# Casts held for a VectorE instruction, and a new work order, in a batched attention kernel

## The chip, the cores and the metric

The kernel runs on one core of a Trainium2 chip. The metric is the device time of one launch in microseconds (us), as the median of several runs; lower is better. The core has five engines with a queue of instructions each, which run beside one another and meet only at semaphores: TensorE (PE; its weight loads are listed as PEld), VectorE (DVE), ScalarE (ACT), GpSimd (POOL) and SyncE (SP), which here only issues transfers.

## The reference

Softmax attention for 8 batches of 8 heads, with 512 queries and keys of 64 elements, in float32:

```python
scale = 1.0 / np.sqrt(q.shape[-1])
scores = np.einsum('bhqd,bhkd->bhqk', q, k) * scale
scores = scores - scores.max(axis=-1, keepdims=True)
attn = np.exp(scores)
attn = attn / attn.sum(axis=-1, keepdims=True)
return np.einsum('bhqk,bhkd->bhqd', attn, v).astype(np.float32)
```

The 64 heads are independent. The kernel does not subtract the maximum; the division by the sum comes at the end.

## The kernel before

**Tiling.** Two heads form a pair, 32 pairs g in all; of each pair q, k and v are loaded as float32 tiles of 128 partitions by 512 elements. Scores are computed transposed: a unit (g, c, h) is a block of 128 keys (chunk c of four) by the 512 queries of head h, so a head has four units and the kernel 256. Of these, 14 (chunk 0 of the first head of the pairs listed in ASIDE) are not given to ScalarE. The other 242 are packed into 83 tiles: the first ones of 1, 1 and 2 units, the last of 1, and 79 of three. A tile is three banks of PSUM, and two such tiles exist (tag `ps_st`).

**The steps.** Each of them is a letter in a string ORDER, which `work` (L333) walks from left to right; each letter issues its instructions to the engines' queues in that order.
- `s`, a tile (L281): three score matmuls on TensorE (L180), one exponential over the tile on ScalarE (L227, `pt<-st`), and, when a pair's first tile is two back, the loads of q and k eight pairs on and of v six pairs on, from SyncE's queue (L97).
- `c`, a cast (L305): on GpSimd, q, then k of a pair to float16 (L115), or v of the pair two before into the value tile `vp` (L121), in a fixed sequence.
- `t`, a turn (L297): eight transposes on TensorE of a pair's cast q and k into one bank of PSUM (L138), and VectorE's copy out of it (L139, `tqk<-tps`).
- `h`, a head (L292): sixteen matmuls on TensorE of the exponentials with the values and a column of ones (L239), then on VectorE the reciprocal of the sums (L252) and the product (L253, `osb<-o,rcp`); after a pair's second head SyncE stores the pair (L261).
- `a`, an aside (L316): one score matmul (L197), and on VectorE the start of an exponential made of arithmetic: an integer part n (L199) and a fraction f (L203, reading PSUM and n). `e` (L323) is its power of two on GpSimd (L207), and `p` (L326) one of three passes on VectorE (L203): `a<-f`, `f<-f,e` and `pa<-a,f`. Each of these passes reads two tensors from SBUF (the first reads f twice). The passes give the unit's weights, which the head of that unit uses last.

**What orders the work.** An engine executes its queue strictly in the order in which ORDER issued it, with no planner at run time. Between engines only data and buffers bind: a turn needs its casts, scores need their turn's copy and a free one of the two score tiles, so the exponential two tiles back; a head needs its exponentials and values. Turns, heads and asides share two banks of PSUM (tag `ps_x`), taken in order, so TensorE can start the next of these only when VectorE has emptied the one two before it. Six value tiles exist, so v of pair g is cast after the heads of pair g - 6. Before ORDER stands a hand-written opening (L340 to L396) for pairs 0 and 1; after it `close` (L275) computes the last head. GpSimd's queue holds only casts and powers, and runs as far ahead as loads and buffers let it.

Of the kernel before, what the change touches and what calls it, by code (L numbers as in the profile page):

```python
# [25 lines left out]

ASIDE = (2, 4, 8, 9, 12, 13, 16, 17, 20, 21, 25, 26, 28, 30)
ORDER = (  # L30
    "csctsccchcacstpshecshpsctchcscccastcepcsctshpcchcstsphcsctpcschccasetshsccpcchhcpshctstacc"
    "shpshstpshhccccstaschesccpaschcepcsctcshscphhpccststesphaschcpsccthsptshscepchaschcsphsttc"
    "cescphpcschapcscchshpccstshpscehashcpshtstcscpthpecshcshtsccphcapccsshhpsctshcccsphceashsp"
    "ccchsttpshaeccshpstcshpshhpscchpsehtsptasshpshhpshcsephhpshshshh"
)


# [1 line left out]
def kernel(  # L39
# [11 lines left out]
    nc = tc.nc  # L51
# [12 lines left out]
    for g in range(n_pairs):  # L64
# [3 lines left out]
        else:  # L68
            units += [(g, c, h) for c in range(NI) for h in range(2)]
    aside = [(g, 0, 0) for g in ASIDE]  # L70
    units = [u for u in units if u not in aside]
# [37 lines left out]
    vps = [cpool.tile([P, 2, NI, W], FP16, name=f"vp{n}") for n in range(NV)]  # L109
    halves, tqk, turned = {}, {}, {}  # L110

    def cast_half(g, n, eng=nc.gpsimd.tensor_copy):
        if g not in halves:
            halves[g] = xpool.tile([P, 2, NI, P], FP16, tag="qk", name=f"qk_{g}", bufs=6)
        eng(  # L115
            out=halves[g][:, n].rearrange("p i (h d) -> p i h d", d=D),
            in_=raw[g, "qk"[n]].rearrange("p h (i d) -> p i h d", d=D),
        )

    def cast_v(g):  # L120
        nc.gpsimd.tensor_copy(  # L121
            out=vps[g % NV][:, :, :, 0:D],
            in_=raw[g, "v"].rearrange("p h (i d) -> p h i d", d=D),
        )

    def aux(shape, dt, name):
        return pspool.tile(shape, dt, tag="ps_x", bufs=2, name=name)

    def transpose(g, parts=(0, 1)):
        if g not in turned:  # L130
            turned[g] = xpool.tile([P, 2, S], FP16, tag="tqk", name=f"tqk_{g}")
            for h in range(2):
                tqk[g, h] = [turned[g][D * h : D * (h + 1), n] for n in range(2)]
        lo, hi = parts[0], parts[-1] + 1
        ps = aux([P, hi - lo, NI, P], FP16, f"tps_{g}_{lo}")
        for n in parts:
            for i in range(NI):
                nc.tensor.transpose(ps[:, n - lo, i, :], halves[g][:, n, i, :], ident16)  # L138
        nc.vector.tensor_copy(out=turned[g][:, lo:hi], in_=ps)  # L139

    N = 2 * NI
    FIRST = NI - 1
# [41 lines left out]
    class Aside:  # L184
# [5 lines left out]
        def __init__(self, unit):  # L190
            self.unit, self.g = unit, unit[0]
            g, c, h = unit
            tq, tk = tqk[g, h]
            n, e, f, a = self.tmp("n", I8), self.tmp("e", I32), self.tmp("f"), self.tmp("a")
            res = self.tmp("pa", FP16)
            s = aux([P, S], FP32, f"sa_{g}")
            nc.tensor.matmul(s, tk[:, c * P : (c + 1) * P], tq, start=True, stop=True)  # L197
            rate = 2.0 * scale * LOG2E
            nc.vector.tensor_scalar(  # L199
                out=n, in0=s, scalar1=rate, scalar2=SHIFT, op0=AluOp.mult, op1=AluOp.add  # L200
            )
            def step(o, x, k, y, op0=AluOp.add, op1=AluOp.mult):
                nc.vector.scalar_tensor_tensor(out=o, in0=x, scalar=k, in1=y, op0=op0, op1=op1)  # L203

            step(f, s, rate, n, AluOp.mult, AluOp.subtract)
            def power():
                nc.gpsimd.tensor_scalar(  # L207
                    out=e,
                    in0=n,
                    scalar1=float(1 << 22),  # L210
                    scalar2=float(LEAD_BITS),
                    op0=AluOp.mult,
                    op1=AluOp.add,
                )

            self.power = power
            self.passes = deque([
                lambda: step(a, f, EXP_P, f),
                lambda: step(f, f, EXP_R, e.bitcast(FP32)),
                lambda: step(res, a, EXP_Q, f),  # L220
            ])
            self.res = res
# [25 lines left out]
    def normalise(g, h, o, lo=0, hi=NI):  # L248
        if g not in o_sb:
            o_sb[g] = opool.tile([P, 2, NI, D], FP32, tag="o_sb", name=f"osb_{g}")  # L250
        rcp = opool.tile([P, NI], FP32, tag="rcp", name=f"rcp_{g}_{h}_{lo}")
        nc.vector.reciprocal(out=rcp[:, lo:hi], in_=o[:, lo:hi, D:W])  # L252
        nc.vector.tensor_tensor(  # L253
            out=o_sb[g][:, h, lo:hi],
            in0=o[:, lo:hi, 0:D],
            in1=rcp[:, lo:hi].broadcast_to([P, hi - lo, D]),
            op=AluOp.mult,
        )

    def save(g, h, n):  # L260
        nc.sync.dma_start(  # L261
# [4 lines left out]
    def attend(g, h):  # L266
        o = aux([P, NI, W], FP32, f"o_{g}_{h}")
        weigh(g, h, o)
        normalise(g, h, o)
        if g == last:  # L270
            save(g, h, 1)
        elif h == 1:
            save(g, 0, 2)

    def close():  # L275
        o = pspool.tile([P, NI, W], FP32, tag="ps_st", bufs=2, name="o_last")
        weigh(last, 1, o)
        normalise(last, 1, o)
        save(last, 1, 1)
# [17 lines left out]
    def turns():  # L297
        for n in range(2):
            transpose(1, (n,))
            yield  # L300
        for g in range(2, n_pairs):
            transpose(g)
            yield

    def casts():  # L305
        for g in range(2, n_pairs + LAG):
            for n in range(2 if g < n_pairs else 0):
                cast_half(g, n)
                yield
            if g >= LAG:  # L310
                cast_v(g - LAG)
                yield
# [19 lines left out]

    def work(order):  # L333
        steps = {k: f().__next__ for k, f in zip("shtca", (tiles, heads, turns, casts, asides))}
        steps |= {"e": next_power, "p": next_pass}
        for k in order:
            steps[k]()

    with tc.manual_schedule():
# [53 lines left out]
        softmax(0)  # L393
        softmax(1)
        cast_half(1, 0, Y)
        cast_half(1, 1, V)  # L396
        work("stst" + ORDER)
        close()

# [28 lines left out]
```

## Time and profile before

| quantity | value |
|---|---|
| median of 5 runs | 121.27 us (120.92 to 121.63) |
| the profiled execution's own time | 121.57 us |
| its span, first to last instruction | 119.8 us |
| ScalarE busy | 111.4 us (93%) |
| TensorE busy, matmuls | 108.1 us (90%) |
| VectorE busy | 102.6 us (86%) |
| GpSimd busy | 71.0 us (59%) |
| read from HBM, written | 25.17 MB, 8.39 MB |
| granted TensorE clock | 1.00 |

How to read the lines. A line of the groups names the source line, the engine, the operation, then out<-in by the program's names, shapes and the number of instructions; behind it stand busy time in us and the mean of one in ns, and behind the last bar the idle time of the engine just before them with what ended it. A line of the waits says which engine at which line waited for what: us in total, times, longest. A line of a timeline has the start and the length in us of one instruction or of a merged run of equal ones, and in brackets idle time before it. The chain of waits is followed back from the last instruction: start, us, what; "issue" is time in which the engine waited for nothing that the profile shows.

### The profile page before, as it was taken

The numbers are of one execution on the slowest core, as the hardware profiler recorded it, in microseconds if no ns is written. First come the engines' busy times: TensorE is split into PE (matmuls) and PEld (weight loads), VectorE is DVE, ScalarE is ACT, GpSimd is POOL, SyncE is SP. The second block draws the span as 40 slices with busy tenths as digits, with TensorE's granted clock in tenths as the row PEclk, the third lists the DMA queues.
The fourth block names the chain that finished last, engine by engine and source line by source line (L and its number), as shares of the span: only waits on it lengthen the run. The fifth ranks groups of instructions, "written<-read, shape, count | busy, mean of one in ns | idle before, by whom it ended". The sixth has DMA issues, their size and how long they took to land.

```text
span 119.8 us, 4065 instructions
## 1 busy us (share of the span) xinstructions
PE 108.1 (90%) x1585; PEld 65.1 (54%) x1585; DVE 102.6 (86%) x246; ACT 111.4 (93%) x88; POOL 71.0 (59%) x114
## 2 busy tenths in 40 slices
PE   6979897989999998999989999999899899979970
PEld 6734554555654645546645565566555566536560
DVE  1354999799999899989999999998999899999870
ACT  4569999999999999999999999999999999999950
POOL 2148899997867869874785577916678424220000
PEclk9999999999999999999999999999999999999999
DMA  3999999999999999999988999899999812404334
GB/s 101 314 345 353 351 346 348 354 376 373 355 356 292 352 360 339 353 376 372 310 262 269 361 345 332 245 358 323 317 333 323 270 47 78 165 5 143 123 109 157
DMA packets 34882, 33.81 MB, mean 282 GB/s; under 512 B 2096, under 2 KB 34864, under 8 KB 34864
## 3 DMA queue, kind: packets, MB, share of 16 engines
q1 hardware_dynamic: 34576, 33.30, 84.8%
q8 instruction: 12, 0.20, 0.7%
q10 hardware_dynamic: 288, 0.26, 0.6%
q14 instruction: 6, 0.05, 0.1%
HBM read 25.17 MB, written 8.39 MB: 280 GB/s over the span
## 4 chain that ended last, share of the span: by engine, by line
ACT 65%; issue 16%; PE 9%; DMA 4%; DVE 1%; SPq 1%; POOL 1%
ACT pt L227 65%; PE o L239 4%; DMA q<-in_q_dram 4%; PE st L180 4%; DVE osb L253 1%; SPq L104 1%; POOL qk L115 1%; DVE rcp L252 0%; PE tps L138 0%
## 5 line engine op out<-in xcount | busy, mean ns | idle before, releaser
L227 ACT ACTIVATE pt<-st 128x1536 f16<-128x1536 f32 (+2 forms) x83 | 109.0, 1496 | 1.5 <-PE st L180 1.2
L180 PE MATMUL st<-tqk 64*128 64x512 f16 x234 | 47.6, 381 | 3.6 <-ACT pt L227 2.5
L239 PEld LDWEIGHTS <-pt 128*128 128x128 f16 x968 | 33.4, 97 | 23.4 <-issue 13.1
L239 PE MATMUL o<-vp,pt 128*128 128x65 f16 x952 | 38.8, 194 | 1.7 <-DVE osb L253 0.6
L121 POOL CAST vp<-v 128x512 f16<-128x512 f32 x32 | 20.9, 655 | 18.3 <-PE o L239 8.5
L253 DVE TENSOR_TENSOR osb<-o,rcp 128x256 f32<-128x256 f32 x63 | 26.8, 425 | 2.2
L115 POOL CAST qk<-q 128x512 f16<-128x512 f32 x31 | 20.6, 663 | 8.3 <-DMA q<-in_q_dram 7.7
L139 DVE COPY tqk<-tps 128x1024 f16<-128x1024 f16 (+1 forms) x32 | 21.3, 669 | 3.2 <-PE tps L138 3.0
L115 POOL CAST qk<-k 128x512 f16<-128x512 f32 x30 | 22.3, 745 | 0.9 <-DMA k<-in_k_dram 0.4
L138 PEld LDWEIGHTS <-qk 128*128 128x128 f16 x248 | 14.4, 97 | 12.9 <-issue 5.4
L138 PE MATMUL tps<-ident,qk 128*128 128x128 f16 x248 | 19.1, 219 | 1.5 <-POOL qk L115 0.7
L180 PEld LDWEIGHTS <-tqk 64*128 64x128 f16 x234 | 11.1, 93 | 11.0 <-issue 3.7
L252 DVE RECIPROCAL rcp<-o 128x4 f32<-128x4 f32 x63 | 11.1, 176 | 3.2 <-PE o L239 2.5
L207 POOL TENSOR_SCALAR e<-n 128x512 int32<-128x512 int8 x14 | 8.7, 620 | 4.8 <-DVE n L199 3.8
L203 DVE SCALAR_TENSOR_TENSOR f<-f,e 128x512 f32<-128x512 f32 x14 | 10.8, 771 | 0.0
L203 DVE SCALAR_TENSOR_TENSOR pa<-a,f 128x512 f16<-128x512 f32 x14 | 10.4, 740 | 0.0
L203 DVE SCALAR_TENSOR_TENSOR f<-sa,n 128x512 f32<-128x512 f32 x14 | 9.7, 691 | 0.5
L203 DVE SCALAR_TENSOR_TENSOR a<-f 128x512 f32<-128x512 f32 x14 | 9.9, 708 | 0.0
L199 DVE TENSOR_SCALAR n<-sa 128x512 int8<-128x512 f32 x14 | 9.5, 681 | 0.0
L197 PE MATMUL sa<-tqk 64*128 64x512 f16 x14 | 5.4, 385 | 0.1
L239 PE MATMUL o<-vp,pa 128*128 128x65 f16 x56 | 4.0, 193 | 0.0
L366 PE MATMUL warm<-blank 128*128 128x128 f16 x25 | 2.8, 313 | 1.0 <-DVE small L348 1.0
(36 smaller groups left out, 23.8 us busy)
## 6 DMA issues: line engine op xcount, KB each, us to landing
v<-in_v_dram SPq DMA_DIRECT2D x32, 256.0 KB, 5.8
q<-in_q_dram SPq DMA_DIRECT2D x31, 256.0 KB, 5.9
k<-in_k_dram SPq DMA_DIRECT2D x31, 256.0 KB, 5.9
out_dram<-osb SPq DMA_DIRECT2D x31, 256.0 KB, 5.3
raw<-in_k_dram ACTq DMA_DIRECT2D x2, 128.0 KB, 3.0
raw<-in_q_dram SPq DMA_DIRECT2D x2, 128.0 KB, 2.8
out_dram<-osb SPq DMA_DIRECT2D x2, 128.0 KB, 1.9
```

The lines of the kernel that those rows point to most:

```text
L115: eng(out=halves[g][:, n].rearrange("p i (h d) -> p i h d", d=D), in_=raw[g, "qk"[n]].rearrange("p h (i d) -> p i h d", d=D),)
L121: nc.gpsimd.tensor_copy(out=vps[g % NV][:, :, :, 0:D], in_=raw[g, "v"].rearrange("p h (i d) -> p h i d", d=D),)
L138: nc.tensor.transpose(ps[:, n - lo, i, :], halves[g][:, n, i, :], ident16)
L139: nc.vector.tensor_copy(out=turned[g][:, lo:hi], in_=ps)
L180: nc.tensor.matmul(st[j][:, x, :], key, tq, start=True, stop=True)
L199: nc.vector.tensor_scalar(out=n, in0=s, scalar1=rate, scalar2=SHIFT, op0=AluOp.mult, op1=AluOp.add)
L203: nc.vector.scalar_tensor_tensor(out=o, in0=x, scalar=k, in1=y, op0=op0, op1=op1)
L207: nc.gpsimd.tensor_scalar(out=e, in0=n, scalar1=float(1 << 22), scalar2=float(LEAD_BITS), op0=AluOp.mult, op1=AluOp.add,)
L227: nc.scalar.activation(out=pt[j][:, 0:n], in_=st[j][:, 0:n], func=EXP, scale=scale)
L239: nc.tensor.matmul(o[:, i, :], p[:, i * P : (i + 1) * P], vps[g % NV][:, h, c, :], start=(c == chunks[0] and i == 0), stop=(c == chunks[-1 ...
L252: nc.vector.reciprocal(out=rcp[:, lo:hi], in_=o[:, lo:hi, D:W])
L253: nc.vector.tensor_tensor(out=o_sb[g][:, h, lo:hi], in0=o[:, lo:hi, 0:D], in1=rcp[:, lo:hi].broadcast_to([P, hi - lo, D]), op=AluOp.mult,)
```

## The change

ASIDE and ORDER are replaced: the 14 units computed aside now belong to other pairs, and the 388 letters stand in another order, with 54 of a new letter `w` among them. All other letters occur as often as before (92 c, 79 s, 63 h, 42 p, 30 t, 14 a, 14 e). A `w` notes the VectorE instruction that was last issued by a turn (its copy), an aside or a pass (its last scalar_tensor_tensor) or a head (its product); the next cast that is issued is made to wait until that instruction is done. A second `w` before that cast replaces the note. Nothing else of the kernel is touched.

```diff
-ASIDE = (2, 4, 8, 9, 12, 13, 16, 17, 20, 21, 25, 26, 28, 30)
+ASIDE = (2, 5, 7, 11, 12, 13, 17, 18, 20, 22, 23, 26, 28, 30)
 ORDER = (
-    "csctsccchcacstpshecshpsctchcscccastcepcsctshpcchcstsphcsctpcschccasetshsccpcchhcpshctstacc"
-    "shpshstpshhccccstaschesccpaschcepcsctcshscphhpccststesphaschcpsccthsptshscepchaschcsphsttc"
-    "cescphpcschapcscchshpccstshpscehashcpshtstcscpthpecshcshtsccphcapccsshhpsctshcccsphceashsp"
-    "ccchsttpshaeccshpstcshpshhpscchpsehtsptasshpshhpshcsephhpshshshh"
+    "cccscscthscasctewcpwschhswccphstwcscpccwtchshashpshcsecctwpwwstcchpshcwstccacscehstwspthcc"
+    "wcpshwcspchtccschaswtccpshcewsacwshwspchwheswptspchwspcchtcsacschpwceshtcpcshshwscpttcwwps"
+    "cwchccshwacecshstchwspchccastwwpsetswwpchshwscphhwpcshcacswscphtespwtcsctswcphchwccspchwaw"
+    "schspehccasscwhwsptcwhwcpstsctwwtcwwcspcheapwcschpshesctschwashcpwststsphhsphewcpwshaeshps"
+    "tshpshphschwcpshphshwcswhhsh"
 )
...
+    latest, held = [], []
+    behind = mybir.DependencyInfo(mybir.DependencyClass.Sync, mybir.DependencyReason.DATA)
+
+    def hold(ins):
+        if held:
+            tc.add_manual_dep(ins.ins, held.pop().ins.name, behind, reason="shared SBUF port")
...
-        eng(
+        ins = eng(
             out=halves[g][:, n].rearrange("p i (h d) -> p i h d", d=D),
             in_=raw[g, "qk"[n]].rearrange("p h (i d) -> p i h d", d=D),
         )
+        hold(ins)
...
-        nc.vector.tensor_copy(out=turned[g][:, lo:hi], in_=ps)
+        latest[:] = [nc.vector.tensor_copy(out=turned[g][:, lo:hi], in_=ps)]
...
-        steps |= {"e": next_power, "p": next_pass}
+        steps |= {"e": next_power, "p": next_pass, "w": lambda: held.__setitem__(slice(None), latest)}
```

`cast_v` gets the same call of `hold`, and the scalar_tensor_tensor of L203 and the product of L253 are noted in `latest` in the same way as the copy.

More of the change, by code (lines that the diff above doesn't have):

```diff
@@ L118, in cast_half @@
         )
+        hold(ins)
     def cast_v(g):
-        nc.gpsimd.tensor_copy(
+        ins = nc.gpsimd.tensor_copy(
             out=vps[g % NV][:, :, :, 0:D],
@@ L124, in cast_v @@
         )
+        hold(ins)
     def aux(shape, dt, name):
@@ L202, in step @@
             def step(o, x, k, y, op0=AluOp.add, op1=AluOp.mult):
-                nc.vector.scalar_tensor_tensor(out=o, in0=x, scalar=k, in1=y, op0=op0, op1=op1)
+                latest[:] = [
+                    nc.vector.scalar_tensor_tensor(
+                        out=o, in0=x, scalar=k, in1=y, op0=op0, op1=op1
+                    )
+                ]
             step(f, s, rate, n, AluOp.mult, AluOp.subtract)
@@ L252, in normalise @@
         nc.vector.reciprocal(out=rcp[:, lo:hi], in_=o[:, lo:hi, D:W])
-        nc.vector.tensor_tensor(
+        latest[:] = [nc.vector.tensor_tensor(
             out=o_sb[g][:, h, lo:hi],
@@ L257, in normalise @@
             op=AluOp.mult,
-        )
+        )]
     def save(g, h, n):
```

## The prediction

> **What bounds the kernel now.** I read the page's table of engines first, then ScalarE's timeline, the groups of instructions, the waits and the chain that ended last. The engine rows leave four candidates:
>
> ```profile
> PE 108.1 (90%) x1585; PEld 65.1 (54%) x1585; DVE 102.6 (86%) x246; ACT 111.4 (93%) x88; POOL 71.0 (59%) x114
> ```
>
> ScalarE's timeline decides between them. From 8.67 us on, its 80 exponentials (79 of three score blocks, one of a single block) make one unbroken piece, and the idle time in brackets lies before its first:
>
> ```profile
> 8.67 106.87 ACT L227 ACTIVATE pt<-st 128x1536 f16<-128x1536 f32 x80 [0.76 <-PE st L180]
> ```
>
> Taken one by one, the large exponentials end 1.343 us apart; only the ones of tiles 22, 58 and 80 come late (1.365, 1.407 and 1.407 us). From the end of tile 3 (10.12) to that of tile 81 (115.05) are 78 steps in 104.93 us, so all lateness together is 104.93 - 78 x 1.3425 = 0.22 us. Between 8.67 and 115.54 us ScalarE is the bound, and there is almost nothing to win back.
>
> What is left to win stands behind it, in the last lines of the chain of waits:
>
> ```profile
> 114.10 0.32 PE st L180
> 114.42 0.61 PE o L239 x16
> 115.03 0.02 issue
> 115.05 0.19 DVE rcp L252
> 115.25 0.02 issue
> 115.27 0.42 DVE osb L253
> 115.69 0.11 DVE rcp L252
> 115.80 0.02 issue
> 115.83 0.42 DVE osb L253
> 116.25 0.10 DVE rcp L252
> 116.35 0.02 issue
> 116.38 0.43 DVE osb L253
> ```
>
> Three heads end one behind the other on VectorE, and the last is done 1.27 us after the last exponential (116.81 against 115.54).
>
> What the change aims at is visible in the groups:
>
> ```profile
> L203 DVE SCALAR_TENSOR_TENSOR f<-f,e 128x512 f32<-128x512 f32 x14 | 10.8, 771 | 0.0
> L203 DVE SCALAR_TENSOR_TENSOR pa<-a,f 128x512 f16<-128x512 f32 x14 | 10.4, 740 | 0.0
> L203 DVE SCALAR_TENSOR_TENSOR f<-sa,n 128x512 f32<-128x512 f32 x14 | 9.7, 691 | 0.5
> L203 DVE SCALAR_TENSOR_TENSOR a<-f 128x512 f32<-128x512 f32 x14 | 9.9, 708 | 0.0
> ```
>
> The three passes that read two SBUF tensors take 681 ns when nothing is in the way. Their means lie 27, 90 and 59 ns above it: 14 x (27 + 90 + 59) = **2.5 us of VectorE** in 13 hit passes. The pass that reads PSUM and one SBUF tensor never moves from 691.
>
> **What the holds do.** Going through the new ORDER letter by letter: 54 w, of which 39 are followed by a cast before the next w (the rest do nothing). The sequence of casts themselves is the same as before; where GpSimd's e stands among them changes. The awaited instruction is a head's product 20 times, a turn's copy 8, a pass 8, an aside's start 3. In 23 of the 39 the next instruction of VectorE is a two-SBUF pass: the pass starts some 35 ns after the awaited one (the gap between neighbours in VectorE's timeline), the released cast comes behind it, and the cast is what waits.
>
> The Trainium skill ("SBUF — State Buffer", Who interferes with whom) says that whoever starts first has the shared pair for the whole instruction and the other fully blocks. The row to weigh it by is the event at 24.6 us, from the timelines of the two engines:
>
> ```profile
> 24.51 0.61 POOL L115 CAST qk<-q 128x512 f16<-128x512 f32 x1
> 25.07 1.07 POOL L115 CAST qk<-k 128x512 f16<-128x512 f32 x1
> ```
>
> The pass began at 24.59 and took 1.07 instead of 0.68 us: of the q cast 0.53 us were left, and 0.39 were added. The k cast then found 0.60 us of the pass left, and 0.45 were added. So blocking is whole, but costs about 0.14 us less than what is left of the other. By the rule a cast released just behind a pass loses about 0.64 us, by the row 0.50; 23 of them 14.7 or 11.5 us of GpSimd, in place of part of the 6.6 us lost now. I take the row. GpSimd goes to some 76 to 79 us busy of 119, which it can bear on average. VectorE gets back 2.5 us at most; the 19 passes without such a hold may be hit as now (2.5 x 19/42 = 1.1), so I take 1.4. An extra wait on GpSimd's queue shows as 17 ns here (the semaphore rows at L115), 0.7 us for 39, inside its slack.
>
> **What that is worth on the path:** close to nothing. VectorE's 1.4 us lies beside ScalarE's unbroken piece; at best it removes the 0.22 us of late exponentials. Without that cover (if VectorE bounded) it would be worth 1.4.
>
> **What is queued behind a held cast.** Everything on GpSimd: the next casts and each aside's power e, which pass two needs; behind the casts the transposes of their pair, and behind those, in TensorE's order, the next scores. I went through the places with the least room, adding starts and durations of rows: scores of a tile 0.53 us from start to the next start, a head 0.60, a turn 0.54, an aside 0.21 on TensorE; a copy 0.69, a head 0.57, an aside 1.33, a pass 0.68 on VectorE; a cast 0.62. Scores can start when the exponential two tiles back ends, and are in time if they start no later than 0.48 us after it.
> - Tiles 20 to 25: v8, k11 and v9 are each released just before a pass. By my sums k11 is cast by 35.25 (transposes reach it at 35.63), k12 by 37.75 (at 38.1): room of 0.35 us. In the same place two heads wait for VectorE to free their PSUM buffer, and tiles 24 and 25 come 0.05 to 0.1 us late.
> - Tiles 54 to 57: three passes, five heads and two asides are 7.55 us for VectorE in four tiles of 1.343; tile 58 some 0.06 us late.
> - Tiles 60 to 66: the densest place. Four passes, four turns, two heads and an aside are 7.95 us in tiles 60 to 63 (before at most 7.7, in tiles 55 to 58, with 0.065 lost). q29, k29 and e come 2.6 us after the awaited copy, just when VectorE wants e. Tiles 65 and 66 up to 0.1 us late.
> - Tiles 78 to 82: v30 and v31 are held until heads 28 and 29, and are ready 0.3 to 1.2 us ahead of their own heads.
>
> Together 0.3 to 0.5 us late, I take 0.4 against 0.22 now: **+0.2**. From below this term is -0.22 (no lateness). From above I find no end short of a stall that repeats: a wait inside TensorE's queue that outlasts 0.48 us goes one to one into the end.
>
> Better than before are tiles 20 to 22, where TensorE had three heads and a turn for two tiles (3.19 us before the next scores, 0.02 late on ScalarE) and now has fewer. The turns come later in the first third (the eighth at tile 18, not 16), which leaves held casts time; in exchange a turn stands two tiles ahead of its first scores, not three.
>
> **Loads and stores.** Their issues stand in SyncE's queue behind the stores, and these wait for the heads (24.0 us for the product, the longest wait 4.4). Heads come up to three tiles sooner in the new order, so most stores are ready sooner; the load that loses most, pair 16's, has a store ahead of it that is two tiles (2.7 us) later than now. Transfers took 5.9 us from issue to landing, and the turn that uses a load stands at least eleven tiles (14.8 us) behind it. Nothing on the path.
>
> **The end.** The old order ends s h h and close, the new one s h and close. Head 30's second half now runs ahead of tile 82. After the last exponential then only four matmuls and one head's division are left: 0.05 us to start, 3 x 0.037 + 0.19 for the four, 0.03 to hand over, and 0.19 + 0.02 + 0.43 for the division, 1.02 us instead of 1.27: **-0.25 us**. From above 0 (if TensorE enters the last five tiles late: its queue there is full, 7.2 to 7.4 us for a room of 7.4), from below -0.35 (the starts in the profile are good to some 0.1). Opening, 0.76 us before tile 3: the code ahead of ORDER is untouched, 0.
>
> **Sum.** Against the profiled execution: span 119.8 us + 0.2 - 0.25 = 119.75, with the 1.77 us around it 121.5 instead of 121.57. That execution lies 0.3 above the median of 121.27; carried over, **121.2**. A measurement of this kernel tells 0.5% (0.6 us) from no change, so this is no change.
>
> **Rivals.**
> - *VectorE is the true limit and the relief counts.* For it: 97.3 us busy in the 105 from 10 to 115 us. Against it: ScalarE's 1.343. Everything at its best is -0.22 - 0.35 = -0.57, 120.7: just short of the bound. 6%, for that and what I may have missed.
> - *Held casts starve TensorE* (tiles 20 to 25, the place with 0.35 us of room). For it: three holds in four casts there, each with a pass behind it, and the waits of before name casts already:
>
> ```profile
> PEld L138 <- POOL qk L115: 5.1, 10, 1.2
> ```
>
> Against: those 5.1 us cost ScalarE next to nothing. If a held cast costs 0.4 us more than summed, three of them make k12 1.2 us late; less the room, 0.85 us go into the end: 122.1. From about 1.0 us later than my sum on, the change is slower by the bound; a like stall at tiles 60 to 66 makes it 122.6 and more. 24%.
> - *The change doesn't do what it says:* the passes stay as long as now, for casts meet them anyway. The time is again 121.2, from the order alone; it lies inside the 70% for no change.
>
> **How the numbers follow.** No change 70% (likeliest, own range 120.8 to 121.7), starved 24%, faster 6%. The range 120.6 to 122.5 leaves out about 5% below and 12% above, the starved case with two stalls.
>
> **What would show it.** Right: exponentials ending 1.343 us apart with 0.3 to 0.5 us lost, at tiles 24, 58 and 65; pass means below 725 in the f<-f,e row; the mean of all casts above 740 (now 686); one head fewer behind the last exponential. Wrong: idle time or steps over 1.5 us on ScalarE, above all with transposes waiting for a cast at 34 to 39 or 86 to 93 us; or, for a gain, a step below 1.34 us.

## The result and the profile after

No difference: 121.67 us against 121.73 us for the kernel before, medians over all their runs; the ratio is **0.9993** (95% interval 0.9979 to 1.0006). The kernel before was at 121.27 us when the prediction was made, and its further runs moved its median up by half a microsecond. What can be compared with the forecast is the ratio: 121.2 for 121.27 was 0.9994.

The engine rows of the changed kernel's page, and ScalarE's timeline:

```profile
PE 106.4 (89%) x1585; PEld 64.7 (54%) x1585; DVE 101.4 (85%) x246; ACT 111.3 (93%) x88; POOL 74.8 (63%) x114
```

```profile
6.33 108.29 ACT L242 ACTIVATE pt<-st 128x512 f16<-128x512 f32 x82 [0.29 <-PE st L375]
```

ScalarE's unbroken piece is there again, now with two more exponentials of the opening in it. The profiled execution is shorter than the one before (span 119.2 against 119.8 us, 120.94 against 121.57 in all), but not for the change. GpSimd's first cast of the pair 1 shows why; kernel before, then the changed one:

```profile
6.81 0.62 POOL L115 CAST qk<-q 128x512 f16<-128x512 f32 x1 [2.11 <-DMA q<-in_q_dram]
```

```profile
5.82 0.62 POOL L124 CAST qk<-q 128x512 f16<-128x512 f32 x1 [1.31 <-DMA q<-in_q_dram]
```

The load of q landed 1.0 us sooner in the second of these executions, in a part of the program that is the same in both, and the gap of 0.76 us ahead of tile 3 (an idle time of ScalarE) closed. So I measure from the end of tile 3's exponential to the end of the last one, which leaves the opening out: **105.42 us before, 105.33 after**. In the measure of the prediction (78 steps of 1.3425), ScalarE was 0.22 us late before and 0.13 after.

The passes, in the groups of the changed kernel:

```profile
L215 DVE SCALAR_TENSOR_TENSOR a<-f 128x512 f32<-128x512 f32 x14 | 9.8, 698 | 0.0
L215 DVE SCALAR_TENSOR_TENSOR pa<-a,f 128x512 f16<-128x512 f32 x14 | 9.7, 691 | 0.0
L215 DVE SCALAR_TENSOR_TENSOR f<-f,e 128x512 f32<-128x512 f32 x14 | 9.7, 690 | 0.0
```

They lose 14 x (17 + 10 + 9) = 0.5 us instead of 2.5, in 6 of 42 passes instead of 13 (a pass counts as hit from 700 ns on). The passes give 2.0 us back to VectorE, and the time does not move. VectorE's row in the page, which counts overlapping neighbours once, falls by 1.2 us, since the records overlap less in the new order.

The end of the chain of waits:

```profile
112.59 1.09 PE o L254 x32
113.67 0.33 PE st L191
114.00 0.00 issue
114.01 0.66 PE o L254 x16
114.67 0.02 issue
114.69 0.20 DVE rcp L267
114.89 0.02 issue
114.91 0.42 DVE osb L268
115.33 0.10 DVE rcp L267
115.44 0.02 issue
115.46 0.43 DVE osb L268
```

One head fewer stands at the end, as foreseen. But the last exponential ends at 114.62, and VectorE is done at 115.89: 1.26 us later, the same as before.

A few executions of most kernels are slow ones, 1.5% or more above its fastest; the ratios leave them out, but the kept profiles of two experiments, "only holds ahead of passes" and "more padding", are such executions, with tiles 4 and 6 late by 1.33 us together, which is taken off in the table below.

### The profile page after: what moved, and what is told of

The parts are those of the page before. It is cut to its first block, busy times and chain, and to the rows that moved or that the text cites. A ratio compares the mean times of both kernels' runs of the same rounds, so it can differ in the third digit from the quotient of the medians.

```text
span 119.2 us, 4083 instructions
## 1 busy us (share of the span) xinstructions
PE 106.4 (89%) x1585; PEld 64.7 (54%) x1585; DVE 101.4 (85%) x246; ACT 111.3 (93%) x88; POOL 74.8 (63%) x114
## 4 chain that ended last, share of the span: by engine, by line
ACT 69%; PE 14%; issue 12%; DVE 1%
ACT pt L242 69%; PE o L254 5%; PE st L191 4%; PE warm L381 2%; PE open L169 1%; DVE osb L268 1%; PE tps L149 0%; PE st L381 0%; DVE rcp L267 0%; PE sa L208 0%; DVE blank L361 0%; DVE small L363 0%; PE open L171 0%; PE st L375 0%
## 5 line engine op out<-in xcount | busy, mean ns | idle before, releaser
L131 POOL CAST vp<-v 128x512 f16<-128x512 f32 x32 | 23.7, 739 | 13.9 <-PE st L191 7.7
L124 POOL CAST qk<-k 128x512 f16<-128x512 f32 x30 | 21.1, 704 | 11.1 <-DVE osb L268 6.6
L124 POOL CAST qk<-q 128x512 f16<-128x512 f32 x31 | 22.5, 726 | 8.2 <-issue 2.7
L215 DVE SCALAR_TENSOR_TENSOR pa<-a,f 128x512 f16<-128x512 f32 x14 | 9.7, 691 | 0.0
L215 DVE SCALAR_TENSOR_TENSOR f<-f,e 128x512 f32<-128x512 f32 x14 | 9.7, 690 | 0.0
```

The source lines that it names most:

```text
L124: ins = eng(out=halves[g][:, n].rearrange("p i (h d) -> p i h d", d=D), in_=raw[g, "qk"[n]].rearrange("p h (i d) -> p i h d", d=D),)
L131: ins = nc.gpsimd.tensor_copy(out=vps[g % NV][:, :, :, 0:D], in_=raw[g, "v"].rearrange("p h (i d) -> p h i d", d=D),)
```

## The experiments

All twelve in one table. "Passes lose" is the sum over the two-SBUF passes of what they took beyond 681 ns, "late" ScalarE's lateness between tiles 3 and 81 against 1.3425 us a tile (not for the shortened exponentials, whose step is shorter), "end" the time from the last exponential to VectorE's last product.

| kernel | ratio to before (95%) | passes lose, hit | late | end |
|---|---|---|---|---|
| before | 1 | 2.5 us, 13 of 42 | 0.22 | 1.26 |
| changed | 0.9993 (0.9979 to 1.0006) | 0.5, 6 | 0.13 | 1.26 |
| new order, no holds | 1.0164 (1.0112 to 1.0215) | 7.0, 24 | 2.89 | 1.26 |
| new order, holds only ahead of passes (23) | 0.9985 (0.9960 to 1.0010) | 2.8, 9 | 0.13 | 1.26 |
| new order, only the other holds (16) | 1.0170 (1.0120 to 1.0220) | 5.9, 22 | 2.27 | 1.26 |
| old order, every cast held | 1.0644 (1.0566 to 1.0723) | 5.0, 21 | 8.61 | 1.26 |
| old order, holds ahead of passes (32) | 1.0106 (1.0076 to 1.0135) | 3.5, 13 | 1.37 | 1.27 |
| before, one pass of three left out | 0.9971 (0.9944 to 0.9998) | 1.9, 8 of 28 | 0.48 | 1.26 |
| changed, small padding | 1.0003 (0.9978 to 1.0029) | none hit | 0.16 | 1.26 |
| changed, more padding | 1.0311 (1.0240 to 1.0383) | none hit | 3.4 | 1.26 |
| changed, two heads sooner | 0.9983 (0.9962 to 1.0004) | 1.0, 8 | 0.37 | 1.26 |
| changed, half of six heads' matmuls | 0.9963 (0.9940 to 0.9987) | 0.5, 6 | 0.06 | 1.03 |
| before, shorter exponentials | 0.9880 (0.9833 to 0.9927) | 3.6, 13 | | 1.37 |
| changed, shorter exponentials | 0.9730 (0.9676 to 0.9783) | 0.7, 7 | | 1.26 |

**The new order without its holds.**

```diff
     def hold(ins):
-        if held:
+        if False:
```

> The changed kernel with its new ASIDE and ORDER, but no cast is made to wait. If ScalarE sets the pace and VectorE's relief is hidden beside it: no difference, 0.998 to 1.003 of the kernel before; the two-SBUF passes lose about 2 us again (0.5 with holds, 2.5 before), ScalarE's lateness between tiles 3 and 81 stays under 0.5 us. If the holds are worth what they give VectorE back (2.0 us) and the new order costs as much: slower by 1 us or more, ratio 1.008 and up.

Measured: 124.13 us, 1.6% slower. The second alternative is met: my reading that the order alone would give the same time falls. The groups of this kernel:

```profile
L215 DVE SCALAR_TENSOR_TENSOR a<-f 128x512 f32<-128x512 f32 x14 | 11.9, 853 | 0.0
L215 DVE SCALAR_TENSOR_TENSOR f<-f,e 128x512 f32<-128x512 f32 x14 | 11.9, 850 | 0.0
L215 DVE SCALAR_TENSOR_TENSOR pa<-a,f 128x512 f16<-128x512 f32 x14 | 11.8, 843 | 0.0
```

The passes lose 7.0 us, nearly three times what they lost in the old order: 32 of the 42 start while GpSimd is at work, against 21 before and 11 with the holds. ScalarE's timeline, one piece before, is in seven pieces, broken for the first time at 37 us; three of them:

```profile
37.55 12.20 ACT L242 ACTIVATE pt<-st 128x1536 f16<-128x1536 f32 x9 [0.59 <-PE st L191]
49.90 13.67 ACT L242 ACTIVATE pt<-st 128x1536 f16<-128x1536 f32 x10 [0.16 <-PE st L191]
63.80 12.44 ACT L242 ACTIVATE pt<-st 128x1536 f16<-128x1536 f32 x9 [0.23 <-PE st L191]
```

The old order keeps casts and passes apart better as it stands; the new one leaves that to its holds. The two parts of the change are worth +1.6% (the order) and -1.7% (the holds in it).

**Every cast of the old order held.**

```diff
-        for k in order:
+        for k in order.replace("c", "wc"):
             steps[k]()
```

(with ASIDE and ORDER of the kernel before)

> The kernel before with its own ASIDE and ORDER, and every one of the 92 casts made to wait for the VectorE instruction issued last before it. If ScalarE sets the pace: passes lose under 0.8 us, more than 40 casts take over 900 ns, GpSimd gets longer by 5 to 10 us, and the time stays within 0.5 us of before. If held casts starve TensorE: lateness on ScalarE of more than 1 us, transposes waiting for casts, 123 us and more.

Measured: 130.06 us. The starved case is met, and it is worse than I had put it: the passes even lose more than without holds (5.0 us), I take it because a cast freed by whatever VectorE instruction was issued last before it starts at no particular distance from a pass; that was not tried apart. From this kernel's waits:

```profile
PEld L148 <- POOL qk L123: 9.3, 16, 1.4
...
ACT pt L241 <- PE st L190: 7.5, 12, 1.3
```

Transposes wait for casts, and ScalarE for scores, as the rival said, at tile 28 (0.60 us late) above all. But not all of the 8.6 us of lateness is of this kind. At tile 32 (1.16 us) and tile 81 (1.39 us) VectorE itself stood idle for 1.02 and 1.56 us until GpSimd had computed a power `e`, and TensorE then waited for VectorE. Tile 34 (1.25 us) has another cause: TensorE worked only 0.46 of the 2 us from 48 to 50 us, and from about 51.6 to 55 us its granted clock was 0.50, in which two heads took 1.94 us instead of 1.09. The mean clock was 0.969 to 0.983 in the three executions behind the ratio, and 0.992 or more in those of the kernel before. The clock in 40 slices of the span, in tenths:

```profile
PEclk9999999999999999599999999999999999999997
```

No other profile of this case has such a slice before its last one. That the pause of TensorE brought the lower clock is not tested; the 6.4% are in any case not the waits for casts alone. The expected relief of the passes did not come.

**One pass less for VectorE.**

```diff
-                lambda: step(a, f, EXP_P, f),
+                lambda: None,
...
-                lambda: step(res, a, EXP_Q, f),
+                lambda: step(res, f, EXP_Q, f),
```

> The kernel before with the first of the three passes of each aside left out (14 passes, 9.9 us of VectorE; the weights of these 14 units are then not the reference's). If ScalarE sets the pace: at most its 0.2 us of lateness goes, ratio 0.997 to 1.000, though VectorE's busy time falls by some 10 us. If VectorE is the limit: 2 us less or more, ratio under 0.985.

Measured: 0.9971, the edge of what was expected if ScalarE sets the pace, and far from 0.985. VectorE's busy time fell from 102.6 to 95.2 us. Its profiled execution was not less late than before (0.48 us), so the small gain isn't pinned to a place. So 7.4 us more for VectorE are worth some 0.3% in the old order (interval 0.02 to 0.56%), and the holds give about a quarter of that time.

**Two heads sooner.**

```diff
-    "tshpshphschwcpshphshwcswhhsh"
+    "tshphsphschwcphsphshwcswhhsh"
```

> The changed kernel with one head's letter moved from tile 77 to 76 and one from tile 79 to 78, so that TensorE has a head less to do from tile 79 on; nothing else moves. If the end is set by TensorE's full queue over the last tiles: TensorE enters tile 80 less than 0.1 us late, and VectorE is done 1.02 us after the last exponential instead of 1.26; 0.24 us less than the changed kernel, ratio near 0.997. If the end is set elsewhere, or the moved heads make a tile late: 1.26 stays, or the gain goes into ScalarE's lateness.

Measured: 1.26 us as before, and tile 79 now 0.30 us late. The last alternative is met. TensorE's timeline of this kernel from tile 78's first head on, its second head at 109.38, and tile 79's scores at 109.98:

```profile
108.65 0.54 PE L254 MATMUL o<-vp,pt 128*128 128x65 f16 x12
109.03 0.28 PE L254 MATMUL o<-vp,pa 128*128 128x65 f16 x4
109.38 0.67 PE L254 MATMUL o<-vp,pt 128*128 128x65 f16 x16
109.98 0.60 PE L191 MATMUL st<-tqk 64*128 64x512 f16 x3
```

From 108.65 to 109.98 are 1.33 us for two heads that take 1.09 elsewhere: the second waits for one of the two shared PSUM banks, and VectorE, with a pass in its queue there, ended its product of the head two before only at 109.33. The moved heads cost what they were to save. That wait I hadn't summed.

**Half of six heads' matmuls left out.**

```diff
+        if 28 <= g <= 30:
+            chunks = chunks[1:3]
```

> The changed kernel with half of the matmuls of the six heads of pairs 28 to 30 left out (their results are then not the reference's): 6 x 0.3 = 1.8 us less for TensorE between tiles 77 and 82. If TensorE's queue sets the end: tile 80 is no longer late, and VectorE is done 1.0 us after the last exponential instead of 1.26, 0.3 us in all. If something fixed lies between the last exponential and the end: 1.26 stays.

Measured: 1.03 us instead of 1.26, tile 80 in time, and 0.4% less than the kernel before (0.9963). VectorE's last four lines, with the last exponential ending at 115.44:

```profile
114.98 0.18 DVE L269 RECIPROCAL rcp<-o 128x4 f32<-128x4 f32 x1 [0.28 <-PE o L256]
115.20 0.42 DVE L270 TENSOR_TENSOR osb<-o,rcp 128x256 f32<-128x256 f32 x1
115.83 0.18 DVE L269 RECIPROCAL rcp<-o_last 128x4 f32<-128x4 f32 x1 [0.20 <-PE o_last L256]
116.05 0.42 DVE L270 TENSOR_TENSOR osb<-o_last,rcp 128x256 f32<-128x256 f32 x1
```

So the 1.02 us that I had worked out exist, once TensorE is ahead of ScalarE. In both real kernels it isn't: when the last exponential ends (114.62 us in the changed one), TensorE is still at the sixteen matmuls of the last head (114.49 to 115.15), and VectorE has two heads to divide.

**VectorE given more to do.** The changed kernel with a memset ahead of each pass, first of 104, then of 250 elements:

```diff
+    idle = cpool.tile([P, 104], FP32, name="idle")
...
         a = passes[0]
+        nc.vector.memset(idle, 0.0)
         a.passes.popleft()()
```

> The changed kernel, holds and all, with a memset of 128x104 float32 on VectorE ahead of each of the 42 passes: some 42 x 0.155 = 6.5 us more for VectorE, as much as the passes lose when the holds are taken out of this order (7.0 against 0.5 us), but no cast meets a pass more than before. If the order without holds is slow because VectorE loses that time: lateness on ScalarE of 2 to 3 us here too, 123.5 to 124.5 us. If it is slow for what the missing holds do to GpSimd or to the order of casts: lateness under 1 us, at most 122.5.

Measured: 1.0003, but the dose was wrong, so this run doesn't decide. A memset took 145 ns, most of it beside its neighbours, and VectorE got 1.4 us busier (102.8), 33 ns for each, not 6.5. It shows only that 1.4 us are borne. (A pass behind a memset takes 628 ns by its record, and none reaches 700.)

> The changed kernel, holds and all, with a memset of 128x250 float32 ahead of each of the 42 passes. The shorter memset (145 ns) made VectorE only 1.4 us busier, for it overlaps its neighbours; this one should take 0.27 us and add 0.13 to 0.16 us each, 5.5 to 6.5 us in all, about what the passes lose without holds (6.5). If that loss is why the order without holds is slow: lateness on ScalarE of 1.5 to 3 us, 123 to 124.5 us. If VectorE can bear it and the slowness comes from GpSimd: under 122.3 us.

Measured: 125.77 us, 1.031. VectorE is 6.4 us busier than in the changed kernel (107.8 against 101.4), no pass is hit, and ScalarE is 3.4 us late. The time went further than the 124.5 that I had set; the direction is the expected one. So time put on VectorE, with all holds in place, makes this order slow without a pass being hit. The run does not isolate that time, though: GpSimd is 5.0 us busier too (79.8 against 74.8), since a cast beside a memset and a pass waits longer, and the transposes' weight loads wait 5.0 us for casts of q and k instead of 3.6. The longest wait on TensorE's side is still for VectorE's products (10.7 us instead of 5.7; 8.6 in the order without holds).

**Which holds count.** Both kernels drop a hold, or keep it, by what VectorE does next:

```diff
-        for k in order:
+        for n, k in enumerate(order):
             steps[k]()
+            if k == "w" and next((x for x in order[n:] if x in "hatp"), "") != "p":
+                held.clear()
```

> The changed kernel with only the 23 holds behind whose awaited instruction VectorE goes on with a pass; the other 16 are dropped. If it is these that protect the passes: they lose under 2 us (0.5 with all holds, 7.0 with none), ScalarE's lateness stays under 0.6 us, 0.998 to 1.004 of the kernel before. If the holds work by spacing GpSimd's queue as a whole: most of the loss comes back, over 1.007.

> The changed kernel with only the 16 holds behind which VectorE goes on with something other than a pass. If the 23 others protect the passes: 4 to 7 us lost by passes and ScalarE late by 1.5 to 3 us, 1.008 to 1.018. If all holds share in it: halfway, some 3 us lost and a lateness near 1 us.

(the second has == for !=.) Measured: with the 23 holds ahead of passes 0.9985, nothing lost; with the other 16 alone 1.017, as slow as with none. The 23 do the work: the 23 passes behind them lose 0.03 us with these holds alone and 4.9 with the others alone, while the remaining 19 passes lose 2.8 and 1.0. The changed kernel's own timelines show how, at 33 us; VectorE, then GpSimd:

```profile
33.17 0.68 DVE L215 SCALAR_TENSOR_TENSOR f<-f,e 128x512 f32<-128x512 f32 x1
```

```profile
33.32 1.01 POOL L124 CAST qk<-k 128x512 f16<-128x512 f32 x1 [0.28 <-DVE osb L268]
```

The cast, freed by the product ahead of the pass, starts 0.15 us behind the pass and pays 0.39 us for it (0.53 us of the pass were left: again 0.14 less); the pass keeps its 0.68. The passes lose 2.8 us without the 16 other holds, against an expected 2 at most, but this costs no time: in this order the loss that hurts begins somewhere between 2.8 and 5.9 us.

**Holds ahead of passes, in the old order.**

```diff
-        for k in order:
+        for k in order.replace("p", "wp"):
             steps[k]()
```

(with ASIDE and ORDER of the kernel before)

> The kernel before with its own ASIDE and ORDER, and a hold on the first cast issued after each place where a pass comes next on VectorE (32 casts). If a hold in front of a pass is all it takes: passes lose under 1 us (2.5 before), ScalarE's lateness stays under 0.5 us and the time within 0.4% of before. If the places must be searched together with the order: some casts are freed too late for their transposes or into a later pass, lateness over 1 us, ratio over 1.008.

Measured: 1.0106. Neither half of the first alternative holds: passes lose 3.5 us, more than without holds, and ScalarE is 1.37 us late. 26 casts take over 900 ns (12 before), so the holds do put casts behind passes, but as many passes are hit as without them. A hold in the right kind of place isn't enough; where the casts behind it then fall was not chosen here.

**ScalarE given less to do.** In each large exponential the last 128 of 1536 columns are left out, and the head's matmuls for them use another unit's weights:

```diff
-        nc.scalar.activation(out=pt[j][:, 0:n], in_=st[j][:, 0:n], func=EXP, scale=scale)
+        to, of = pt[j][:, 0:n], st[j][:, 0:n]
+        if n == G:
+            to = to.rearrange("p g s -> p (g s)")[:, 0 : G * S - P]
+            of = of.rearrange("p g s -> p (g s)")[:, 0 : G * S - P]
+        nc.scalar.activation(out=to, in_=of, func=EXP, scale=scale)
...
                 p = pt[j][:, x]
             for i in range(NI):
+                if p is not apart.get((g, c, h)) and x == G - 1 and i == NI - 1:
+                    p = pt[j][:, 1]
```

> The kernel before with 128 of the 1536 columns left out of each of the 79 large exponentials (in their place the weights of another unit are used, so the results are not the reference's): 79 x 0.107 = 8.4 us less for ScalarE. If ScalarE alone sets the pace, 8.4 us less, 113.3. VectorE's queue (some 104 us of work with the gaps between instructions, 2.5 of them lost to casts, from 8 us on) says 114 to 116; its instructions then run with under 0.05 us a tile between them, and ScalarE is idle for 2 us or more.

> The changed kernel with the same 128 columns left out of each of the 79 large exponentials. If what the holds give back is hidden only by ScalarE, it shows here: 1.5 to 2 us less than the kernel before with the same columns left out. If TensorE or waits inside the order come next: the two are within 0.7 us of each other.

Measured: 120.78 us for the old kernel so shortened, 118.49 for the changed one; from tile 3's exponential to the last 104.45 and 102.33 us. The old kernel hardly uses its shorter exponentials (1.0 us of 8.4): the 113.3 of ScalarE alone is out, and even the 114 to 116 of VectorE's sum was too low. ScalarE's group in the two, old kernel first:

```profile
L231 ACT ACTIVATE pt<-st 128x1408 f16<-128x1408 f32 (+2 forms) x83 | 103.2, 1317 | 6.5 <-PE st L180 5.4
```

```profile
L246 ACT ACTIVATE pt<-st 128x1408 f16<-128x1408 f32 (+2 forms) x83 | 103.2, 1318 | 3.7 <-PE st L191 2.6
```

ScalarE waits for scores 5.4 us in one, 2.6 in the other. The changed kernel is 2.1 us shorter over the stretch and 2.3 in all, against 3.6 - 0.7 = 2.9 us that its passes lose less there. So a gain of the change is there, and ScalarE hides it. What of it comes from the holds and what from the new order was not tried apart here; nor is it known what stops the changed kernel from using more than 3.0 of the 8.4 us.

## Where the prediction held, and which of its steps failed

**No change, and ScalarE as the reason, held.** ScalarE's piece is unbroken in both kernels, its lateness of 0.22 us was all that VectorE's relief could win, and with shortened exponentials a gain of the change comes out. But the sum behind the forecast failed in three of its steps: the end, the lateness, and the absolute time.

**The end, -0.25 us: wrong, 0.** "After the last exponential then only four matmuls and one head's division are left" fails: most of the last head's sixteen matmuls and two divisions were left. From 106 us on TensorE's queue is full. Its timeline runs without a break from tile 77's scores to the last head. First and last line of that stretch, before, then changed:

```profile
106.97 0.59 PE L180 MATMUL st<-tqk 64*128 64x512 f16 x3 [0.16 <-ACT pt L227]
115.41 0.66 PE L239 MATMUL o_last<-vp,pt 128*128 128x65 f16 x16
```

```profile
106.06 0.59 PE L191 MATMUL st<-tqk 64*128 64x512 f16 x3 [0.16 <-ACT pt L242]
114.49 0.66 PE L254 MATMUL o_last<-vp,pt 128*128 128x65 f16 x16
```

That is 106.97 to 116.06 and 106.06 to 115.15, 9.09 us both times, with the same ten heads in it. The new order moves a head ahead of the last tile's scores, but inside this stretch: those scores start 7.54 us into it instead of 7.06, still in time for ScalarE, whose last exponential ends 8.56 us into it (8.57 before). The work of TensorE that is left then is the same. I had named 0 as the upper bound of the term and had still taken -0.25. Taking matmuls out of this stretch gave 1.03 us behind the last exponential, as worked out; so the full queue is the cause, and the room that I had counted on was not there. The scores of tiles 80 and 81 also take 0.75 us from start to the next start, not 0.53: in the lists of the last pair all units of one head stand together, elsewhere the two heads alternate. That this order of units is the cause is argued, not tried.

**Lateness, +0.2 us: wrong, -0.09.** The step that failed is the walk through tiles 20 to 25. There k12 was cast by 36.6 us, not 37.75; about 0.8 us of that is the sooner opening of the execution, and the three freed casts ahead of it lost 0.33, 0.39 and 0.24 us, not 0.50 each. Tile 58, late before, and tile 65 were in time as well; no tile but 80 was late by more than 0.03 us.

**The absolute time, 121.2 us: measured 121.67.** The sum was carried over to a median of five executions, 121.27, from which the profiled one was said to lie 0.3 us above. Over 80 executions the median is 121.73, and the profiled one lies 0.16 us below it. This reference accounts for nearly all of the 0.47 us; the change itself was put at -0.07 and measured -0.06.

The two wrong terms of the change are of like size and opposite sign (+0.2 and -0.25, measured -0.09 and 0), so that it came out right is partly luck.

**The relief** was put at 1.4 us of VectorE and measured 2.0; the term mis-sized was the 19 passes without a hold ahead, put at 1.1 us and measured 0.4. What a freed cast pays was taken from the row as 0.50 us; most of the 23 casts over 900 ns pay 0.33 to 0.40 (946 to 955 and 1002 to 1011 ns against 616), since a released cast starts 0.15 us or more behind its pass and I had put it right behind. GpSimd came to 74.8 us busy, just under the 76 to 79, and the mean of all casts to 723 ns, where over 740 was named as a sign.

**"The order alone gives the same time" was wrong** by 2.4 us. I treated the order as neutral, having looked for overloaded stretches with passes at 681 ns, and never asked how often they would be hit in this order if casts ran free.

**The starved rival** did not come about in the change. Holds on all casts of the old order cost 6.4%, with waits for casts and powers in it, and a stretch at half clock.

## What to carry to other kernels

Time given back to an engine is worth at most what the bounding engine waits for it, here 0.22 us of 2.0; before shortening something, sum up how late the pacing engine is against its own step. Two changes made together can each be large: measure them apart before calling either neutral, and ask of a new order what it would cost without the guard that came with it. At the end of a kernel count a full queue's work from the last point at which it waited, and not from the last exponential. And carry a forecast over as a ratio: the median of five executions was off by more than the change.

## What the runs showed that I had not expected

- A load that is the same in both kernels lands at different times from one execution to the next: the first q of pair 1 is cast from 5.8 to 7.1 us on in these profiles. Between the two main profiles that moved the opening by 0.8 us, more than the change did. It isn't the only thing that moves there: with that cast at 5.79 us in one profile and 5.82 in another, tile 3's exponential ended at 9.95 and 9.29.
- In the new order VectorE bears a loss up to a point: with 0.5 and 2.8 us lost by its passes ScalarE was 0.1 us late, with 5.9 and 7.0 us 2.3 and 2.9 us. As an estimate from these four profiles, some 3 us are free, and of the next 4 each costs about 0.7 us. The holds differ between them too, and in the old order 3.5 us lost went with 1.4 us of lateness, so this is no rule for other orders.
- A wait makes a good separator of two engines that block each other: the three casts freed ahead of a pass between 31 and 35 us of the changed kernel started 0.15 to 0.30 us behind the pass, which kept its 0.68 us.
